# Last expert of a mixture-of-experts kernel: the last up stage behind two down stages, and row statistics taken half by half

## The chip, the cores and the metric

The kernel runs on one core of a Trainium2 chip. The metric is the time of the whole program on the device in microseconds, the median of several runs. The profile shows one further execution of the same program.

## What is computed

Two transformer layers on 256 tokens of 1024 features. The first has a gated delta network and a dense feed-forward part; the second has windowed attention and a mixture of eight experts. The change lies in the mixture and in the layer norm behind it. Of the reference, what matters is:

```python
for e in range(N_EXPERTS):                      # 8 experts, EXPERT_DIM = 3584
    h = jax.nn.silu(xf @ w_gate[e]) * (xf @ w_up[e])
    out = out + gates[:, e:e + 1].astype(xf.dtype) * (h @ w_down[e])
...
x = layer_norm(ALPHA * x + f, ln_g[i, 1], ln_b[i, 1])
```

The gates of a token are nonzero for the two experts with the largest router logits.

## The kernel before

All matmuls of the experts work on weights in fp32, each of which is split on the core into a rounded part `hi` and a remainder `lo`. The function `unit` does this for one piece of 1 MB: a transfer from the SyncE queue into a `raw` buffer (line 145), a cast to `hi` on ScalarE (line 154), and the subtraction `lo = raw - hi` on VectorE (line 155). `raw` buffers come from a ring, of which eight are in use in the last expert; `hi` and `lo` have four buffers each.

Up to 128 tokens are gathered for each expert. Its 3584 inner features are worked on in seven blocks of 512, numbered 0 to 6 (`NB` is 7). A block has a gate stage, an up stage and a down stage, and each of these stages needs two units of weights. The blocks go in pairs, (0,1), (2,3), (4,5), and the last alone. The list `stages` holds the order: gate and up of a pair, then the down stages of the pair before it, then an entry "held" that does the work which needs the finished gate and up sums. So the last expert ends with

```python
gate 6, up 6, down 4, down 5, held 6, down 6      # and then finish(7)
```

`work` is the same list without the "held" entries. Each stage first calls `loads` for the next stage of `work`, so weights are asked for one stage ahead. In the up stage the gate sum goes through Silu on ScalarE into `msg` (line 1363). Where an expert has at most 64 tokens, which is the branch that these runs take from the second expert on (`light` in `arms`), the `hi` and `lo` parts of the tokens lie side by side (`xp`, `hp`), the matmul of line 1205 does both, and the two halves of a sum are added by a copy `low` (line 1199) and a matmul with `fold` (line 1195). `multiply` forms `msg * up` on VectorE (line 1329); `turned` transposes the product on TensorE (line 1253), casts it to `hT` on ScalarE (1256), subtracts on VectorE (1257) and packs both into `hp` on ScalarE (1118, 1119), which the down stage reads. `turn_one` does this for one block of the list `held`.

The results of the other experts are gathered into `yt` (line 1292, POOL queue) and added to `y` on VectorE (line 1294) by `collect`; its second half is called with `issue_after(subs[-1].ins)`, which puts it behind the last subtraction written so far on VectorE. `finish` adds the last expert to `y` without that detour: casts `yh`, subtractions `yl`, matmuls with `PT` (1285, 1286), and four updates of `y` (1288), one for each block of 128 tokens and each half of the features. Then a branch follows (`tc.If(cv > P)`, line 1404), for experts with more than 128 tokens, which these runs don't enter. Behind it come the row statistics of `y` (`bn_stats` 1470, `bn_aggr` 1471), the reciprocal root, and the scaled output in four pieces.

The order of instructions on each engine is set when the program is built: by the order in which they are written, by the buffers that are free, and by a planner's own costs.

Of the kernel before, what the change touches and what calls it, by code (L numbers as in the profile page):

```python
# [23 lines left out]
F32 = mybir.dt.float32  # L24
# [6 lines left out]
P = 128  # L31
# [8 lines left out]
NE = 8  # L40
# [42 lines left out]
def kernel(ctx: ExitStack, tc: tile.TileContext, A, out):  # L83
    nc = tc.nc
    V, S, G, PE = nc.vector, nc.scalar, nc.gpsimd, nc.tensor
# [999 lines left out]
    def at(j, tb):  # L1085
        return bass.IndirectOffsetOnAxis(ap=keyi[:, j, tb:tb + 1], axis=0)

    with ExitStack() as mctx:
        ylng = [raw_in(per, t) for t in ("Bh", "lngb")]
        turns = more_ring(mctx, "ring_m", 2, [raw_in(per, t) for t in ("Al", "Bl", "Ah")] + ylng)  # L1090
# [139 lines left out]
        def down(e, b, hT, us, then=lambda: None):  # L1230
            if b == 0:
                acc[e] = [accb() for _ in range(2)]

            def heavy():
                for u, (wh, wl) in enumerate(us):
                    for h in range(2):
                        mm3(acc[e][h], lambda k: hT[0][:, 0, (2 * u + k) * P:(2 * u + k + 1) * P],
                            lambda k: hT[0][:, 1, (2 * u + k) * P:(2 * u + k + 1) * P],
                            [(wh[:, k, h * 512:(h + 1) * 512], wl[:, k, h * 512:(h + 1) * 512]) for k in range(2)],
                            b == 0 and u == 0, b == NB - 1 and u == 1)  # L1240

            def light():
                for u, ws in enumerate(us):
                    for h in range(2):
                        mm2(acc[e][h], hT[1], 2 * u, [[w[:, k, h * 512:(h + 1) * 512] for k in range(2)] for w in ws],
                            b == 0 and u == 0, b == NB - 1 and u == 1)
                then()
            arms(e, heavy, light)
# [23 lines left out]
        def finish(e):  # L1272
            PT = mp.tile([P, T], F32R, name="PT", bufs=1)
            p = trb()
            for tb in range(2):
                PE.transpose(p[:, tb * P:(tb + 1) * P], Pe[e][:, tb, :], ident)
            S.copy(PT, p[:, :T])
            for h in range(2):
                yh = mp.tile([P, 512], F32R, name="yh", tag="msg")
                yl = mp.tile([P, 512], F32R, name="yl", tag="low")  # L1280
                S.copy(yh, acc[e][h])
                V.tensor_sub(yl, acc[e][h], yh.bitcast(F32))
                for tb in range(2):
                    p = trb()
                    PE.matmul(p, PT[:, tb * P:(tb + 1) * P], yh, start=True, stop=False)
                    PE.matmul(p, PT[:, tb * P:(tb + 1) * P], yl, start=False, stop=True)
                    ys = y[tb][:, h * 512:(h + 1) * 512]
                    V.scalar_tensor_tensor(ys, p, gate[:, tb, e:e + 1], ys, op0=OP.mult, op1=OP.add)

        def collect(j, tb):  # L1290
            yt = per.tile([P, D], F32, name="yt", tag="x%d" % tb)
# [13 lines left out]
        def loads(what, e, b):  # L1305
            if what == "down":
                behind[0] = None
                v = wd_[e].rearrange("(f p) n -> p f n", p=P)
                return [unit(v[:, 4 * b + 2 * u:4 * b + 2 * u + 2, :], 2, D) for u in range(2)]
            w = (wg_ if what == "gate" else wu_)[e]  # L1310
            behind[0] = placed if (e, b) == (0, 1) or (e, b, what) == (0, 0, "up") else None
            if b == NB - 1:
                return colunits(w, 512 * b, 512)
            k0, c0 = 4 * (b % 2), 1024 * (b // 2)
            v = w.rearrange("(k p) n -> p k n", p=P)
            return [unit(v[:, k0 + 2 * u:k0 + 2 * u + 2, c0:c0 + 1024], 2, 1024) for u in range(2)]

        work = [s for s in stages if s[0] != "held"]
        nexts = iter(work[1:])
        hT, held, mine, late, kept = {}, [], [], [], None  # L1320
        ready = {work[0]: loads(*work[0])}

        def turn_one():
            e, b, s = held.pop(0)
            hT[e, b] = turned(s, e)
# [6 lines left out]

        for what, e, b in stages:
            if what != "held":
                nxt = next(nexts, None)
                quanta[0] = 1 if e or b > 1 else 4
                if nxt:
                    ready[nxt] = loads(*nxt)
                us = ready.pop((what, e, b))
            whole = b == NB - 1 or b % 2  # L1340
            if what == "gate":
                if b % 2 == 0:
                    pgs = [mm() for _ in range(1 if whole else 2)]
                gateup(e, b, us, pgs)
                if b % 2 == 0 and b < NB - 1:
                    multiply()
                elif held:
                    turn_one()
                if whole:
                    lgs_ = [low(p) if e else None for p in pgs]  # L1350
                if kept is not None and (e, b) == (kept[0] + 1, 2):
                    next(kept[1], None)
                    kept = None
            elif what == "up":
                if b % 2 == 0:
                    pus = [up() for _ in range(1 if whole else 2)]
                gateup(e, b, us, pus, lambda: [addlow(p, l) for p, l in zip(pgs, lgs_)] if whole else None)
                if held:
                    turn_one()
                if whole:  # L1360
                    for n, (pg, pu) in enumerate(zip(pgs, pus)):
                        s_ = mp.tile([P, 512], F32, name="msg", tag="msg")
                        S.activation(s_, pg, AF.Silu)
                        mine.append((b - len(pgs) + 1 + n, pu, low(pu) if e else None, s_, e))
                if b == 1 and e + 1 < NE:
                    fetch(e + 1)
                if b == 5 - 2 * (e > 0) and e + 1 < NE:
                    xg[e + 1] = gather(e + 1)
            elif what == "held":
                if e:  # L1370
                    arms(e, lambda: None, lambda: [addlow(pu, lu_) for _, pu, lu_, _, _ in mine])
                if b == NB - 2 or (e, b) == (NE - 1, NB - 1):
                    multiply()
                if (e, b) == (NE - 1, NB - 1):
                    turn_one()
                if (e, b) == (NE - 2, NB - 1):
                    turns.remove(ylng[0])
                    yy = per.tile([P, 2, D], F32, name="y", tag="Bh")
                    for tb in range(2):
                        y.append(yy[:, tb])  # L1380
                        nc.gpsimd.dma_start(y[tb], x3d[tb * P:(tb + 1) * P])
                        G.tensor_scalar(y[tb], y[tb], ALPHA, None, op0=OP.mult)
                if e == NE - 1 and b > 1:
                    with tc.issue_after(subs[-1].ins):
                        for c in late:
                            next(c, None)
                    late = [collect(b // 2 - 1, tb) for tb in range(2)] if b < NB - 1 else []
                    for c in late:
                        next(c)
                if (e, b) == (NE - 1, 1):  # L1390
                    turns.remove(ylng[1])
                    lnp = ln_params(3, nc.gpsimd)
                if (e, b) == (NE - 1, 5):
                    onehot(e, True)
            else:
                down(e, b, hT.pop((e, b)), us)
                if b == NB - 1 and e < NE - 1:
                    kept = (e, keep(e))
                    next(kept[1])
        finish(NE - 1)  # L1400


    cv = nc.values_load(cnti[0:1, 0:1], min_val=0, max_val=T)
    with tc.If(cv > P):
        with tc.For_i(0, E, 1) as ei, ExitStack() as octx:
# [51 lines left out]
            for h in range(2):  # L1457
                S.copy(y2[:, h * 512:(h + 1) * 512], ya[h])
                for tb in range(2):
                    p = trb()  # L1460
                    PE.matmul(p, PT2[:, tb * P:(tb + 1) * P], y2[:, h * 512:(h + 1) * 512], start=True, stop=True)
                    ys = y[tb][:, h * 512:(h + 1) * 512]
                    V.scalar_tensor_tensor(ys, p, pse[:, 2, tb:tb + 1], ys, op0=OP.mult, op1=OP.add)

    g, b = lnp
    mv = small.tile([P, 2, 2], F32, name="fin_mv")
    for tb in range(2):
        st = small.tile([P, 2, 6], F32, name="ln_st")
        for h in range(2):
            V.bn_stats(st[:, h, :], y[tb][:, h * 512:(h + 1) * 512])  # L1470
        V.bn_aggr(mv[:, tb, :], st)  # L1471
    ve, rs = (small.tile([P, 2], F32, name="fin_" + n) for n in ("ve", "rs"))
    V.tensor_scalar(ve, mv[:, :, 1], LN_EPS, None, op0=OP.add)  # L1473
    rsqrt(rs, ve, [P, 2])
# [29 lines left out]
```

## Time and profile before

| | |
|---|---|
| time, median of 3 runs | 1416.77 us (1416.58 to 1417.6) |
| profiled execution, its own time | 1412.96 us |
| its span | 1411.3 us |
| mean granted TensorE clock | 0.988 of full speed |
| busy share PE, PEld, DVE, ACT, POOL | 93%, 74%, 83%, 72%, 5% |

The span is what the profile covers; the profiled execution's own time also has what lies around it. PE is TensorE's matmuls, PEld its weight loads, DVE VectorE, ACT ScalarE, POOL GpSimd, SP SyncE; a "q" behind the name is the engine's queue of transfers. Times in rows are counted from the start of the span.

### The profile page before, as it was taken

What the parts mean: (1) busy time and instruction counts of PE and PEld (TensorE: products, weight loads), DVE (VectorE), ACT (ScalarE), POOL (GpSimd) and SP (SyncE); (2) the same over time, 40 slices, a digit from 0 to 9 for tenths busy, and PEclk for the clock granted to TensorE, in tenths of its full rate; (3) what the DMA queues carried; (4) which work ended last, traced back from release to release, by engine and by line L of the source; (5) the groups of instructions that cost most, each with busy time, mean ns of one, the idle gap of its engine ahead of it and who ended that gap; (6) DMA issues with size and microseconds to landing.
All of it is one profiled execution on the core that took longest, in us unless ns stands there. A gap on an engine that the chain in (4) does not pass through costs nothing. (4 is left out here: it accounts for less than half of the span.)

```text
span 1411.3 us, 17398 instructions
## 1 busy us (share of the span) xinstructions
PE 1309.4 (93%) x6175; PEld 1042.5 (74%) x6175; DVE 1165.8 (83%) x1300; ACT 1013.4 (72%) x1264; POOL 67.3 (5%) x90
## 2 busy tenths in 40 slices
PE   7999999999999999988999999998989999888884
PEld 5889788888777888766677777776667776666662
DVE  4885975554877898889988888889998889999998
ACT  4763544444364577799888878789988888998983
POOL 4000000000000320000000000000000000002110
PEclk9999999999999899999999999999999999999998
DMA  8641576764643899999999999999999999999992
GB/s 272 199 151 61 180 260 220 236 209 151 203 174 117 306 421 415 362 397 404 419 410 378 353 368 359 359 372 409 405 419 416 357 375 380 395 414 418 419 416 80
DMA packets 145378, 446.76 MB, mean 317 GB/s; under 512 B 12704, under 2 KB 20032, under 8 KB 145264
## 3 DMA queue, kind: packets, MB, share of 16 engines
q1 hardware_dynamic: 137072, 420.64, 78.3%
q0 software_dynamic: 5280, 18.66, 3.5%
q10 hardware_dynamic: 2912, 5.90, 1.3%
q8 instruction: 76, 1.25, 0.3%
q14 instruction: 38, 0.31, 0.1%
HBM read 435.05 MB, written 15.36 MB: 319 GB/s over the span
## 5 line engine op out<-in xcount | busy, mean ns | idle before, releaser
L155 DVE TENSOR_TENSOR lo<-raw,hi 128x2048 fp32r<-128x2048 f32 (+1 forms) x610 | 910.2, 1534 | 115.8 <-ACT hi L154 111.8
L154 ACT CAST hi<-raw 128x2048 fp32r<-128x2048 f32 (+1 forms) x610 | 769.5, 1312 | 152.5 <-PE acc L171 59.1
L1205 PE MATMUL acc<-lo,xp 128*128 128x512 f32 x224 | 74.6, 420 | 18.7 <-DVE lo L155 16.4
L170 PE MATMUL acc<-hi,hT 128*128 128x512 f32 x224 | 88.4, 395 | 2.0 <-ACT hi L154 2.0
L170 PE MATMUL mm<-hi,xg 128*128 128x512 f32 x224 | 87.5, 392 | 0.5 <-ACT low L1199 0.5
L170 PE MATMUL acc<-hi,xg 128*128 128x512 f32 x224 | 88.0, 393 | 0.0
L171 PE MATMUL mm<-hi,xg 128*128 128x512 f32 x224 | 87.3, 390 | 0.0
L171 PE MATMUL acc<-hi,hT 128*128 128x512 f32 x224 | 87.3, 390 | 0.0
L171 PE MATMUL acc<-hi,xg 128*128 128x512 f32 x224 | 87.2, 389 | 0.0
L1205 PE MATMUL mm<-lo,xp 128*128 128x512 f32 x224 | 70.7, 403 | 10.2 <-DVE lo L155 10.1
L1205 PE MATMUL acc<-lo,hp 128*128 128x512 f32 x224 | 71.5, 400 | 4.5 <-DVE lo L155 4.4
L1205 PEld LDWEIGHTS acc<-lo,xp 128*128 128x128 f32 x224 | 38.8, 190 | 45.1 <-DVE lo L155 39.1
L1205 PE MATMUL acc<-hi,hp 128*128 128x512 f32 x224 | 70.7, 397 | 1.2 <-ACT hp L1119 1.2
L1205 PE MATMUL mm<-hi,xp 128*128 128x512 f32 x224 | 68.7, 393 | 2.2 <-ACT low L1199 1.5
L1205 PE MATMUL acc<-hi,xp 128*128 128x512 f32 x224 | 69.7, 398 | 0.0
L173 PE MATMUL acc<-lo,hT 128*128 128x512 f32 x224 | 69.0, 389 | 0.0
L173 PE MATMUL acc<-lo,xg 128*128 128x512 f32 x224 | 67.7, 389 | 0.0
L173 PE MATMUL mm<-lo,xg 128*128 128x512 f32 x224 | 67.7, 389 | 0.0
L1329 DVE TENSOR_TENSOR msg<-msg,acc 128x512 f32<-128x512 f32 x56 | 36.5, 684 | 36.0 <-PEq L1189 33.1
L1205 PEld LDWEIGHTS mm<-lo,xp 128*128 128x128 f32 x224 | 40.3, 188 | 27.3 <-DVE lo L155 19.9
L1118 ACT CAST hp<-tr 128x256 fp32r<-128x256 f32 x49 | 19.0, 387 | 55.0 <-DVE hT L1257 54.9
L1253 PE MATMUL tr<-ident,msg 128*128 128x128 f32 x224 | 34.9, 284 | 22.6 <-DVE msg L1329 22.6
(410 smaller groups left out, 2325.6 us busy)
## 6 DMA issues: line engine op xcount, KB each, us to landing
raw<-in_moe_w_gate_dram SPq DMA_DIRECT2D x112, 1024.0 KB, 7.8
raw<-in_moe_w_up_dram SPq DMA_DIRECT2D x112, 1024.0 KB, 7.5
raw<-in_moe_w_down_dram SPq DMA_DIRECT2D x112, 1024.0 KB, 8.0
raw<-in_a_w_in_dram SPq DMA_DIRECT2D x12, 1024.0 KB, 5.6
raw<-in_ffn_w_gate_dram SPq DMA_DIRECT2D x11, 1024.0 KB, 5.0
raw<-in_ffn_w_up_dram SPq DMA_DIRECT2D x11, 1024.0 KB, 5.1
raw<-in_ffn_w_down_dram SPq DMA_DIRECT2D x11, 1024.0 KB, 4.9
raw<-in_b_w_in_dram SPq DMA_DIRECT2D x5, 1024.0 KB, 5.1
```

The lines of the kernel that those rows point to most:

```text
L154: S.copy(hi[:, c], raw[:, c])
L155: subs.append(V.tensor_sub(lo[:, c], raw[:, c], hi[:, c].bitcast(F32)))
L170: PE.matmul(ps, xh(k), wh, start=first and k == 0, stop=False)
L171: PE.matmul(ps, xl(k), wh, start=False, stop=False)
L173: turn[0] = PE.matmul(ps, xh(k), wl, start=False, stop=last and k == n - 1)
L1118: S.copy(v[:, :, 0], p)
L1205: PE.matmul(ps, x[:, (k0 + i % n) * P:(k0 + i % n + 1) * P], w, start=first and i == 0, stop=last and i == 2 * n - 1)
L1253: PE.transpose(p[:, f * P:(f + 1) * P], s[:, f * P:(f + 1) * P], ident)
L1329: V.tensor_mul(s_, s_, pu)
```

## The change

In the last expert the up stage of block 6 is taken out of its place and put behind the down stages of blocks 4 and 5: gate 6, down 4, down 5, up 6, held 6, down 6. The order in which weights are asked for is changed as well: gate 6, down 4, down 6, down 5, up 6, so the two units of down 6 are split ahead of those of down 5, and up 6's come last of all. Since `work` no longer has the order of `stages`, the loop asks for weights until those of the stage at hand are there. Both blocks 4 and 5 are turned in the gate stage, and the second pair of `y` additions from `collect` is written behind the down stage of block 5. The `bn_stats` of `y` are written directly behind each update of `y`, in `finish` and in the branch that isn't entered, and `bn_aggr` stands ahead of the branch (and at its end). A tile `st` and a small unused tile join the pool `rt`.

```diff
+    mv = small.tile([P, 2, 2], F32, name="fin_mv")
+    st = rt.tile([P, 2, 2, 6], F32, name="fin_st")
+    rt.tile([P, 8], F32, name="pad")
...
                     V.scalar_tensor_tensor(ys, p, gate[:, tb, e:e + 1], ys, op0=OP.mult, op1=OP.add)
+                    V.bn_stats(st[:, tb, h, :], ys)
...
+        end = NE - 1, NB - 1
+        at_up = stages.index(("up",) + end)
+        stages.insert(at_up + 2, stages.pop(at_up))
         work = [s for s in stages if s[0] != "held"]
+        work.insert(-2, work.pop())
...
             if what != "held":
-                nxt = next(nexts, None)
                 quanta[0] = 1 if e or b > 1 else 4
-                if nxt:
-                    ready[nxt] = loads(*nxt)
+                while True:
+                    nxt = next(nexts, None)
+                    if nxt:
+                        ready[nxt] = loads(*nxt)
+                    if (what, e, b) in ready:
+                        break
                 us = ready.pop((what, e, b))
...
                 elif held:
+                    turn_one()
+                if (e, b) == end:
                     turn_one()
...
                 down(e, b, hT.pop((e, b)), us)
+                if (e, b) == (NE - 1, NB - 2):
+                    with tc.issue_after(subs[-1].ins):
+                        for c in late:
+                            next(c, None)
+                    late = []
...
         finish(NE - 1)
+
+    def means():
+        for tb in range(2):
+            V.bn_aggr(mv[:, tb, :], st[:, tb])
+
+    means()
...
                     V.scalar_tensor_tensor(ys, p, pse[:, 2, tb:tb + 1], ys, op0=OP.mult, op1=OP.add)
+                    V.bn_stats(st[:, tb, h, :], ys)
+        means()
...
-    mv = small.tile([P, 2, 2], F32, name="fin_mv")
-    for tb in range(2):
-        st = small.tile([P, 2, 6], F32, name="ln_st")
-        for h in range(2):
-            V.bn_stats(st[:, h, :], y[tb][:, h * 512:(h + 1) * 512])
-        V.bn_aggr(mv[:, tb, :], st)
```

## Rows read from the trace of the kernel before

In rows of instructions the columns are: start, length in us from the first start to the last end, engine, line, operation, output and inputs, and in brackets the engine's idle time before it and what ended it.

**Rows 1.** The page, busy time of each engine over the span with its share and its number of instructions.

```profile
PE 1309.4 (93%) x6175; PEld 1042.5 (74%) x6175; DVE 1165.8 (83%) x1300; ACT 1013.4 (72%) x1264; POOL 67.3 (5%) x90
```

**Rows 2.** Busy time by stretch, near the end: stretch, its length, busy us of PE, PEld, DVE, ACT, POOL with numbers of instructions, granted clock, share of the transfer engines, GB/s.

```profile
1360.00:1380.00 20.00, 14.96 (x63) 10.78 (x61) 20.00 (x19) 13.83 (x14) 4.22 (x2) 1.00 1.01 411
1380.00:1400.00 20.00, 12.86 (x53) 8.96 (x53) 18.71 (x21) 9.14 (x12) 0.00 (x0) 0.95 0.03 11
```

**Rows 3.** The last run of weight transfers that the SyncE queue issues, in order of time, and a shorter stretch of the table by stretch.

```profile
1354.07 13.17 SPq L145 DMA_DIRECT2D raw<-in_moe_w_down_dram  x6
...
1380.00:1384.00 4.00, 2.76 (x14) 2.11 (x15) 4.00 (x5) 4.00 (x5) 0.00 (x0) 1.00 0.12 47
```

**Rows 4.** VectorE in order of time, 1366 to 1393.

```profile
1366.76 2.48 DVE L1294 SCALAR_TENSOR_TENSOR y<-yt,gat,y 128x1024 f32<-128x1024 f32 x2
...
1372.06 2.29 DVE L155 TENSOR_TENSOR lo<-raw,hi 128x2048 fp32r<-128x2048 f32 x1
...
1382.38 0.69 DVE L1329 TENSOR_TENSOR msg<-msg,acc 128x512 f32<-128x512 f32 x1
...
1387.38 0.70 DVE L1257 TENSOR_TENSOR hT<-tr,hT 128x512 fp32r<-128x512 f32 x1
1387.98 2.29 DVE L155 TENSOR_TENSOR lo<-raw,hi 128x2048 fp32r<-128x2048 f32 x1
1390.18 2.49 DVE L1294 SCALAR_TENSOR_TENSOR y<-yt,gat,y 128x1024 f32<-128x1024 f32 x2
```

**Rows 5.** TensorE's matmuls in order of time: the last up stage (1372 to 1376) and the last down stage (1388 to 1393).

```profile
1372.07 1.19 PE L1205 MATMUL acc<-lo,xp 128*128 128x512 f32 x4 [3.06 <-DVE lo L155]
...
1374.40 1.19 PE L1205 MATMUL acc<-lo,xp 128*128 128x512 f32 x4 [0.22 <-DVE lo L155]
1375.44 0.40 PE L1195 MATMUL mm<-low,fold 128*128 128x512 f32 x1
...
1388.84 0.73 PE L1205 MATMUL acc<-hi,hp 128*128 128x512 f32 x2 [1.20 <-ACT hp L1119]
1389.41 0.63 PE L1205 MATMUL acc<-lo,hp 128*128 128x512 f32 x2
...
1392.15 0.62 PE L1205 MATMUL acc<-lo,hp 128*128 128x512 f32 x2
```

**Rows 6.** ScalarE in order of time: an `hT` cast of an earlier block, a weight cast, and the way of the last up stage.

```profile
1304.12 0.59 ACT L1256 CAST hT<-tr 128x512 fp32r<-128x512 f32 x1 [0.93 <-PE tr L1253]
...
1371.63 1.94 ACT L154 CAST hi<-raw 128x2048 fp32r<-128x2048 f32 x1
...
1380.03 0.60 ACT L1363 ACTIVATE msg<-mm 128x512 f32<-128x512 f32 x1
1380.51 0.59 ACT L1199 CAST low<-acc 128x512 fp32r<-128x512 f32 x1
...
1388.11 0.37 ACT L1118 CAST hp<-tr 128x256 fp32r<-128x256 f32 x1 [0.82 <-DVE hT L1257]
1388.38 0.41 ACT L1119 CAST hp<-hT 128x256 fp32r<-128x256 f32 x1
```

**Rows 7.** TensorE and VectorE in order of time: an addition of `low` that had to wait for it, the step from two additions over two multiplies to transposes, and the last transposes of a product.

```profile
1305.25 0.50 PE L1195 MATMUL acc<-low,fold 128*128 128x512 f32 x1 [0.34 <-ACT low L1199]
...
1357.80 0.61 PE L1195 MATMUL acc<-low,fold 128*128 128x512 f32 x2
...
1358.36 1.28 DVE L1329 TENSOR_TENSOR msg<-msg,acc 128x512 f32<-128x512 f32 x2
...
1359.10 1.25 PE L1253 MATMUL tr<-ident,msg 128*128 128x128 f32 x8 [0.69 <-DVE msg L1329]
...
1383.12 0.66 PE L1253 MATMUL tr<-ident,msg 128*128 128x128 f32 x4 [1.12 <-DVE msg L1329]
```

**Rows 8.** The tile `yt` from 1290 on: the gathers on POOL (their length as minimum, median and maximum in ns, first and last start) and the time from an issue of this tile's transfers to landing.

```profile
L1292 POOL DMA_INDIRECT yt<-ys,keyi x4: 1751/1922/2470, 1316.6 to 1370.4; - x4
...
DMA to landing us min/median/max: 7.5/8.9/9.9
```

**Rows 9.** VectorE in order of time, from the updates of `y` in `finish` to the last scale.

```profile
1394.03 1.40 DVE L1288 SCALAR_TENSOR_TENSOR y<-tr,gate,y 128x512 f32<-128x512 f32 x2
1395.66 1.41 DVE L1288 SCALAR_TENSOR_TENSOR y<-tr,gate,y 128x512 f32<-128x512 f32 x2 [0.23 <-PE tr L1286]
1397.97 1.88 DVE L1470 BATCH_NORM_STATS2 ln_st<-y 128x6 f32<-128x512 f32 x3 [0.90 <-DVEq L1404]
1399.77 0.19 DVE L1471 BATCH_NORM_AGGREGATE fin_mv<-ln_st 128x2 f32<-128x12 f32 x1
...
1400.44 0.73 DVE L1478 SCALAR_TENSOR_TENSOR y<-y,fin_mv,lngb 128x512 f32<-128x512 f32 x1
...
1405.31 2.74 DVE L1479 SCALAR_TENSOR_TENSOR y<-y,fin_rs,lngb 128x512 f32<-128x512 f32 x4
```

**Rows 10.** Busy time by stretch where the granted clock (the third column from the right) fell: columns as in Rows 2.

```profile
28.00:30.00 2.00, 0.00 (x0) 0.00 (x0) 0.00 (x0) 0.00 (x0) 1.49 (x7) 0.81 0.10 36
...
462.00:464.00 2.00, 1.08 (x5) 1.11 (x6) 1.95 (x6) 0.00 (x0) 0.27 (x1) 0.69 1.03 406
```

**Rows 11.** TensorE in order of time: the first matmuls behind these two gaps.

```profile
30.14 1.02 PE L429 MATMUL acc<-g__261,cst 128*128 128x8 f32 x4 [3.44 <-POOL g__261 L425]
...
462.92 1.94 PE L1003 MATMUL tr<-ident,x 128*128 128x128 f32 x8 [2.46 <-DVE x L312]
```

## The prediction

> **What bounds the kernel now.** I read the page first: over the whole span TensorE (PE) has the largest busy share, 93% [rows 1], which alone would suggest counting matmuls. But the change touches only the last expert, so I went to the busy time by stretch of the last 70 us [rows 2]. There the picture turns over: from 1360 on VectorE (DVE) is busy 20.00 of 20 us and then 18.71 of 20, while PE falls to 14.96 and 12.86. The transfers are nearly as full as DVE up to 1380 and then stop: the share is 1.01, then 0.03. So the next question was when the last weights arrive. The SyncE queue issues its last run of weights in a stretch that ends at 1367.24, and the DMA share has fallen to 0.12 over 1380 to 1384 [rows 3]: the last weights are there at about 1381. The last `lo` subtraction (line 155), however, runs at 1387.98 and ends at 1390.27 [rows 4]. DVE is some nine microseconds behind the memory. In the end stretch the stream of `lo` subtractions on DVE, one of about 2.2 us for each unit of weights (start to start; 2.29 us each), sets the pace, and PE waits for them (3.06 us before the last up stage) [rows 5].
>
> What follows the last subtraction is short. The last down stage is 16 matmuls from 1388.84 to 1392.77 [rows 5]; they were released by the casts of `hp` at 1388.79 [rows 6], and the last `lo` is needed only near their end. So from the end of the last subtraction to the end of the last down matmul pass only 1392.77 - 1390.27 = 2.50 us. Two down stages' worth of subtractions hide the long way from the last up stage to `hp`: on DVE the multiply `msg` (line 1329) stands at 1382.38 and the `hT` subtraction at 1387.38, among the weights [rows 4].
>
> **Part 1, the order of stages and weights.** Number of matmuls, casts, subtractions and weight transfers is unchanged, and the transfers' 1 MB units are equal, so the SyncE queue does the same waits at the same slots and the last landing stays at about 1381. What changes is what is last: now the two units of the last up stage. After their last subtraction nothing may start until this chain is through, and no weights are left to hide it. Each link from its own row:
>
> 1. Four `lo` matmuls and the addition of the gate's `low`. Today the subtraction at 1372.06 ends at 1374.35 [rows 4] and the addition (line 1195) ends at 1375.84 [rows 5]: 1.49 us.
> 2. Silu and the cast of `low` on ScalarE, one behind the other: 1380.03 to 1381.10, 1.07 us [rows 6]; with a release of about 0.08 us, 1.15.
> 3. Addition of the up `low`: 0.05 us of release and 0.50 [rows 7]: 0.55.
> 4. Multiply: 0.69 us [rows 4]. The pair of multiplies at 1358.36 starts 0.17 us after the first of its two additions must have ended (1357.80 + 0.39) [rows 7], so 0.87 with that release.
> 5. Four transposes: from the multiply's end at 1383.07 to 1383.12 + 0.66: 0.71 [rows 4, 7].
> 6. `hT` cast 0.59 us with 0.03 of release [rows 6]: 0.62; `hT` subtraction 0.70 [rows 4] with 0.04: 0.74.
> 7. `hp`, two casts, 1388.08 to 1388.79 [rows 4, 6]: 0.71.
> 8. The 16 down matmuls, 1388.79 to 1392.77 [rows 5, 6]: 3.98.
>
> Sum: 10.82 us, against 2.50 today: **+8.32**. The cover of links 2 to 7 was DVE's and ScalarE's work on down weights; with it gone they cost their full length.
>
> The subtraction stream itself also moves. On DVE, which takes its instructions in order, the multiply (0.60 from start to start) and the `hT` subtraction (0.60) leave the stream for the chain behind it; the second pair of `y` accumulations (line 1294, 1390.18 to 1392.57, 2.39) [rows 4] is put behind the subtractions of the second down stage, and so ahead of the last up stage's two, which queue behind it. Their gather is issued at 1370.4 on POOL and done issuing at about 1372.8, and that isn't moved; with up to 9.9 us to land [rows 8] it is ready at about 1382.7, ahead of its new place at about 1384.6. Net **+1.19**. From below: if the accumulations fall into the chain's idle time after all, the stream gains 1.20 instead, but then a slot wait appears (next paragraph), and the net is about 0. I take +1.19, since the first pair, too, stands today where it is written, at 1366.76 and ahead of the up stage's subtractions [rows 4].
>
> Slots: `hi` and `lo` have four buffers each, and the weights of the last down stage now hold two until the end. The last up's units must wait until the second down stage has read its own. After the first of that stage's subtractions, six matmuls of 0.23 us [rows 5] and a cast of 1.94 us [rows 6] make 3.4 us before the first up subtraction can begin. Behind it on DVE stand one subtraction (2.2) and the accumulations (2.39), 4.6 us together: covered. Without the accumulations it would be a wait of 1.2 us. Two `hT` instead of one are turned in the gate stage; their work is the same and its place is not on the last path. I take 0.
>
> **Part 2, row statistics.** The four `bn_stats` after the branch (three take 1.88 us from 1397.97) [rows 9] move behind each `y` update in `finish`. They were and are on DVE, on the path. Before: first update at 1394.03 to start of the scale by `rs` at 1405.31, 11.28 us [rows 9], of which 0.23 is a wait for PE and 0.90 the branch. After: four updates of 0.66 and four statistics of 0.605 start to start, 5.06; two aggregates 0.30; the branch 0.90; the rest of the chain 4.87 (1400.44 to 1405.31) less one aggregate, 4.76. Sum 11.02: **-0.26**. The branch cannot be hidden by it. Bounds: 0 if the branch takes longer, -1.5 if the statistics fit into waits.
>
> **Sum.** 8.32 + 1.19 - 0.26 = +9.25. The profiled execution took 1412.96 us (span 1411.3), so 1422.2; its time stands 3.8 us under the median of the runs, 1416.77, which gives **1426.0**.
>
> **Rivals.**
>
> *A. The clock falls in the new gap (slower still).* Between the last up matmuls and the down matmuls PE now has about 1.2 us of work in 5.3. The granted clock fell from full speed, 2.4 GHz, towards 1.2 GHz (a mean of 0.81 over 28 to 30) after PE had been idle for 3.44 us up to 30.14, and it fell between 462 and 464, after small matmuls and 2.46 us of idleness [rows 10, 11]. Against it: it stayed at 1.00 through the idle 3.06 us before the last up stage (no stretch from 1360 to 1380 is lower) and through 1380 to 1384 with 2.76 of 4 us busy [rows 2, 3, 5]. If it falls, the 16 matmuls at 0.228 from start to start (twelve in 2.74 us) [rows 5] take twice that, +3.65, and the last few of `finish` some 0.35: 1430.0. The Trainium skill ("TensorE: Matmul & The Clock Gate", "HAM oscillation") says that a matmul burst after an idle wait starts at the low clock and that each such burst pays; by that rule the sum would be this rival's 1430.0 and not 1426.0. The rows above show both outcomes after gaps of this size.
>
> *B. Slots run short.* If ScalarE's queue delays the casts of the last units (it already waits for DVE's `hT` subtractions ahead of `hp`) [rows 6], the waits bounded at 1.2 us above come on top, at most twice that with the accumulations: 1427.2 to 1428.4.
>
> *C. Not slower: PE's waits were the loss.* From 1368 on PE stands idle for 3.06 us before the up stage and for 1.20 us before the last down stage [rows 5]. If both go because down matmuls fill them, and the end is PE's, the time is 1416.8 - 4.3 - 0.3 = 1412.2. That needs the last subtraction to end some 13.5 us earlier than I have it (9.25 + 4.3), at about 1378, before the last weights have landed (1381). Even if DVE followed the memory at once, landing at 1381, a cast, a subtraction and 10.82 us of chain end at 1396, still 3.3 us behind today's 1392.77. What would save it is that the chain is shorter than its links, below 7.5 us, as well as DVE free.
>
> *D. The order isn't followed.* The order on each engine is set when the kernel is built, and not as written throughout: the eight transposes of two blocks run in one piece at 1359.10 [rows 7], where the code asks for one block in the gate stage and for the other in the up stage. If the up weights are still split ahead of the down weights, the time stays at about 1416.5. Against it: there are only four buffers and the down weights ask first.
>
> **Chances and range.** My sum 0.55; A 0.22; B 0.09; C 0.06; D 0.08. That gives faster 0.06, same (within 0.2%, 2.8 us, about what measurement can tell from no change) 0.08, slower 0.86. My sum's own uncertainty is -2.5 (statistics in waits, accumulations in the gap) to +1.5. The range reaches over A: 1420.0 to 1431.5, and on the low side some way towards D.
>
> **What would show it.** In the profile after: the last line-155 subtraction belongs to an up stage and ends at about 1391.5; DVE is then idle for more than 2 us before a lone multiply; the last 16 down matmuls begin about 6.8 us later and end near 1402; the clock there is 1.00 (sum) or 0.50 (A); no `bn_stats` stands behind the branch. The prediction is wrong if the subtraction stream ends before 1385, if the chain's links overlap with weight work, or if DVE waits ahead of the last two units (B).

## The result

The changed kernel takes 1435.93 us (median; 1435.25 to 1436.71) against 1416.67 of the kernel before in the same comparison: 1.0146 times the time, with a 95% interval of 1.0123 to 1.0169. That is 19.3 us slower, where 9.25 were forecast, and 4.4 us above the range. The two profiled executions stand further apart than the medians, 1411.3 and 1434.9 us of span, since that of the kernel before lay 3.7 us under its median and that of the changed kernel 0.8 over its own; so positions are compared within the profiles below, and prices by medians.

The page of the changed kernel, span and busy times; [rows 1] is the second line's counterpart:

```profile
span 1434.9 us, 17394 instructions
...
PE 1331.2 (93%) x6175; PEld 1049.9 (73%) x6175; DVE 1166.3 (81%) x1300; ACT 1012.0 (71%) x1264; POOL 64.8 (5%) x90
```

The number of instructions on TensorE and VectorE is the same to the piece. VectorE's busy time is the same to half a microsecond. TensorE's has grown by 21.8 us with the same 6175 matmuls: they last longer. The next views say which.

**First place: long before the edited stages.** VectorE in order of time, four multiplies `msg` in the middle of the program, first in the kernel before:

```profile
690.82 0.68 DVE L1329 TENSOR_TENSOR msg<-msg,acc 128x512 f32<-128x512 f32 x1
...
936.17 0.69 DVE L1329 TENSOR_TENSOR msg<-msg,acc 128x512 f32<-128x512 f32 x1 [2.88 <-PEq L1189]
...
1044.48 0.68 DVE L1329 TENSOR_TENSOR msg<-msg,acc 128x512 f32<-128x512 f32 x1
...
1273.78 0.68 DVE L1329 TENSOR_TENSOR msg<-msg,acc 128x512 f32<-128x512 f32 x1
```

and the same four multiplies in the changed kernel:

```profile
694.36 0.68 DVE L1338 TENSOR_TENSOR msg<-msg,acc 128x512 f32<-128x512 f32 x1
...
945.15 0.69 DVE L1338 TENSOR_TENSOR msg<-msg,acc 128x512 f32<-128x512 f32 x1 [3.41 <-PEq L1192]
...
1053.57 0.68 DVE L1338 TENSOR_TENSOR msg<-msg,acc 128x512 f32<-128x512 f32 x1
...
1285.62 0.68 DVE L1338 TENSOR_TENSOR msg<-msg,acc 128x512 f32<-128x512 f32 x1
```

The changed kernel is late by 3.54, 8.98, 9.09 and 11.84 us. On every engine the instructions stand in the same order in both kernels up to the last expert, so nothing was moved there. Most of the lag grows in some experts only: the trace has matmuls with `xg` and `hT`, the branch for more than 64 tokens, in experts 0, 2, 3 and 5, and there it grows, by 10.7 us in all; with `xp` and `hp`, in experts 4, 6 and 7, it stays to within 0.2. (Ahead of the prediction it is said that these runs take the short branch from the second expert on. That was wrong: four of the eight take the long one.)

In expert 1, a short one, the lag grows by 1.67 us too, and that has nothing to do with the change. It is TensorE's clock, first in the kernel before, then in the changed one (columns as in [rows 2]):

```profile
608.00:610.00 2.00, 2.00 (x10) 1.65 (x10) 2.00 (x2) 0.17 (x1) 0.00 (x0) 1.00 1.04 420
```

```profile
608.00:610.00 2.00, 2.00 (x6) 1.52 (x6) 2.00 (x2) 1.06 (x1) 0.00 (x0) 0.52 0.95 332
```

Of all the traces of this case only that of the kernel before has full speed there; the others, also those in which nothing is displaced, lose 1.5 to 1.7 us at this place. Ahead of the first expert the changed kernel is 0.8 us early. So 10.7 of the 11.84 are the experts of the long branch, and the rest lies between these two executions.

TensorE's matmuls by line and operands in the stretch 820 to 920, which lies in such experts; the last figures before the idle time are busy us and mean ns. The kernel before:

```profile
L171 PE MATMUL acc<-hi,xg 128*128 128x512 f32 x48 | 18.7, 389 | 0.0
...
L171 PE MATMUL acc<-hi,hT 128*128 128x512 f32 x40 | 15.6, 390 | 0.0
```

The changed kernel:

```profile
L171 PE MATMUL acc<-hi,xg 128*128 128x512 f32 x48 | 18.9, 393 | 0.0
...
L171 PE MATMUL acc<-hi,hT 128*128 128x512 f32 x39 | 15.3, 393 | 0.0
```

The same matmul lasts a little longer. From start to start, over all neighbouring matmuls with `xg` in the trace, the median went from 227 to 232 ns (means 227.1 and 232.6), and with `hT` likewise. An expert of the long branch has 42 units with 12 matmuls each, 504 x 0.0055 = 2.8 us; the lag grows by 2.6 to 2.7 in each of the four.

**Second place: the end.** VectorE in order of time in the changed kernel, to be read against [rows 4, 9]:

```profile
1370.20 1.28 DVE L1338 TENSOR_TENSOR msg<-msg,acc 128x512 f32<-128x512 f32 x2
...
1396.42 2.47 DVE L1298 SCALAR_TENSOR_TENSOR y<-yt,gat,y 128x1024 f32<-128x1024 f32 x2
1398.82 4.70 DVE L155 TENSOR_TENSOR lo<-raw,hi 128x2048 fp32r<-128x2048 f32 x2
1406.84 0.69 DVE L1338 TENSOR_TENSOR msg<-msg,acc 128x512 f32<-128x512 f32 x1 [3.33 <-PE acc L1198]
1408.90 0.69 DVE L1260 TENSOR_TENSOR hT<-tr,hT 128x512 fp32r<-128x512 f32 x1 [1.37 <-ACT hT L1259]
...
1417.92 1.40 DVE L1291 SCALAR_TENSOR_TENSOR y<-tr,gate,y 128x512 f32<-128x512 f32 x2
...
1428.97 2.74 DVE L1500 SCALAR_TENSOR_TENSOR y<-y,fin_rs,lngb 128x512 f32<-128x512 f32 x4
```

The order is as written: the second pair of sums `y`, the two subtractions of the last up stage, then a lone multiply behind 3.33 us of idle time. The multiply of blocks 4 and 5 at 1370.20 stood at 1358.36 before [rows 7]: that is the lag of 11.84 that the kernel brings into its end. TensorE in order of time over the same stretch, against [rows 5]:

```profile
1403.57 1.21 PE L1208 MATMUL acc<-lo,xp 128*128 128x512 f32 x4 [0.29 <-DVE lo L155]
1404.61 0.40 PE L1198 MATMUL mm<-low,fold 128*128 128x512 f32 x1
1406.26 0.47 PE L1198 MATMUL acc<-low,fold 128*128 128x512 f32 x1 [1.26 <-ACT low L1202]
1407.59 0.66 PE L1256 MATMUL tr<-ident,msg 128*128 128x128 f32 x4 [0.85 <-DVE msg L1338]
...
1410.35 1.22 PE L1208 MATMUL acc<-hi,hp 128*128 128x512 f32 x2 [1.89 <-ACT hp L1122]
...
1415.57 0.62 PE L1208 MATMUL acc<-hi,hp 128*128 128x512 f32 x2
1416.03 0.63 PE L1208 MATMUL acc<-lo,hp 128*128 128x512 f32 x2
```

and busy time by stretch there, columns as in [rows 2]:

```profile
1406.00:1408.00 2.00, 0.89 (x5) 0.60 (x6) 0.69 (x1) 0.12 (x1) 0.00 (x0) 1.00 0.00 0
1408.00:1410.00 2.00, 0.46 (x5) 0.22 (x3) 0.69 (x1) 1.24 (x4) 0.00 (x0) 0.66 0.00 0
1410.00:1412.00 2.00, 1.65 (x4) 1.36 (x5) 0.00 (x0) 0.30 (x1) 0.00 (x0) 0.50 0.00 0
```

Between the last up matmuls and the down matmuls TensorE has short pieces of work with waits of 1.26, 0.85 and 1.89 us between them, and in the last of these the granted clock goes from 1.00 to 0.50, 1.2 GHz. The down matmuls begin at half speed and end at full speed: 1410.35 to 1416.66, 6.31 us, where [rows 5] show 3.93.

Measured from the multiply of blocks 4 and 5, the last subtraction ends 1.41 us later than before (1403.52 - 11.84 = 1391.68, against 1390.27). From there to the end of the last down matmul pass 13.14 us instead of 2.50, +10.64. From there to the end of the span (1434.91, and 1411.26 before) pass 18.25 instead of 18.49, -0.24. Together +11.81 for the end, and with the 11.84 that came before it 23.65, the difference of the spans.

### The profile page after: what moved, and what is told of

It is laid out like the page before. It is cut to its first block, busy times and chain, and to the rows that moved or that the text cites. A ratio compares the mean times of both kernels' runs of the same rounds, so it can differ in the third digit from the quotient of the medians.

```text
span 1434.9 us, 17394 instructions
## 1 busy us (share of the span) xinstructions
PE 1331.2 (93%) x6175; PEld 1049.9 (73%) x6175; DVE 1166.3 (81%) x1300; ACT 1012.0 (71%) x1264; POOL 64.8 (5%) x90
## 5 line engine op out<-in xcount | busy, mean ns | idle before, releaser
L1208 PE MATMUL acc<-lo,hp 128*128 128x512 f32 x224 | 75.1, 418 | 8.0 <-DVE lo L155 7.9
L1208 PE MATMUL acc<-hi,hp 128*128 128x512 f32 x224 | 75.1, 418 | 4.3 <-ACT hi L154 2.4
L1208 PEld LDWEIGHTS acc<-lo,hp 128*128 128x128 f32 x224 | 42.9, 198 | 24.7 <-DVE lo L155 15.5
```

The lines of the kernel that those rows point to most:

```text
L1208: PE.matmul(ps, x[:, (k0 + i % n) * P:(k0 + i % n + 1) * P], w, start=first and i == 0, stop=last and i == 2 * n - 1)
```

## The experiments

In the expectations S is the theory that a shift of addresses did it, D that any displacement does, M that matmuls are slowed by where their stationary operand lies, O that the new order of stages did, W that the order of weights did, A that the low clock did, and R that executions just differ. The kernel before, run beside each, took 1414.2 to 1415.1 us.

**What moves up when `st` and the unused tile join the pool `rt`.** They take 96 and 32 bytes of each partition, 128 together, and pools opened later lie above them. By the addresses given when the program is built, `xg` went from 180736 to 180864, `hT` from 201728 to 201856, `xp` and `hp` likewise, and the ring `ring_m` too; `hi`, `lo` and `raw`'s other ring stayed. Before, these were multiples of 256 bytes (and of 512), and then odd multiples of 128. So the first kernel is the one before with 128 bytes more in `rt` and nothing else:

```diff
+    rt.tile([P, 32], F32, name="pad")
     with ExitStack() as mctx:
```

> The kernel before with one unused tile of 128 bytes per partition in the pool rt, and nothing else: every tile of the pools above it (ring_m, moe) lies 128 bytes higher, as in the changed kernel, and the order of all instructions is that of before. Theory S (the shift of addresses costs the 7 to 12 us that the changed kernel has lost before the last expert's tail begins): 1424 to 1428.5 us, matmuls of the experts slower by some 2%, the last part as before. Rival O (the reordered stages cost it all, in a way that shows before them): 1416.7 us. Rival R (the executions differ among themselves, not the programs): 1416.7 us as well, with the kernel before drifting by several us.

Measured: 1424.41 us, 1.0075 [1.0049, 1.0100], +10.2. In its trace the lag grows by 10.8 us in the experts of the long branch, and stands at 10.25 at the multiply of blocks 4 and 5. An unused tile makes about half of the loss.

Next, the 128 bytes between the ring and the experts' own pool, so that only the latter moves:

```diff
     turns = more_ring(mctx, "ring_m", ...)
+    mctx.enter_context(tc.tile_pool(name="between", bufs=1)).tile([P, 32], F32, name="pad")
```

> The kernel before with 128 unused bytes between the pools ring_m and moe: only the tiles of moe (xg, hT, xp, hp, low, msg) lie 128 bytes higher, the raw buffers where they were. Theory M (the matmuls are slowed by the place of their stationary operands xg and hT): all of the loss of the run with both pools moved, some 10 us above before, 1424 us; matmuls with xg and hT again 1 to 2% longer. Rival W (the weights' way, that is transfers into and reads out of the moved raw buffers): no change from before, about 1414.3 us.

Measured: 1424.45 us, 1.0071 [1.0047, 1.0096]. The whole loss comes from the pool that holds `xg`, `xp`, `hT` and `hp`; the ring has no part in it.

The first edit with 512 and with 256 bytes instead of 128:

```diff
+    rt.tile([P, 128], F32, name="pad")     # the second kernel: [P, 64]
```

> The kernel before with 512 unused bytes in the pool rt, so ring_m and moe lie 512 bytes higher. In the kernel before, every moe tile that TensorE reads starts at a multiple of 512 bytes of its partition, in the changed kernel none does. Theory M with alignment (what counts is whether the 512 bytes that one weight load takes from a partition straddle such a boundary): as before, about 1414.3 us. Rival D (any displacement of these pools costs): some 1424 us.

> The kernel before with 256 unused bytes in the pool rt: the moe tiles lie at odd multiples of 256 bytes. If the boundary that counts is one of 512 bytes, every weight load of 512 bytes a partition straddles one again, and the loss is that of the 128-byte run, about 10 us: 1424 us. If multiples of 256 are enough, no change: 1414.5 us. If the loss grows with the part that lies beyond the boundary, more than 10 us.

Measured: 1415.15 us, 1.0009 [0.9993, 1.0025], with 512, and 1414.97, 0.9999 [0.9989, 1.0010], with 256. So it isn't displacement as such, and multiples of 256 are enough, where I had supposed 512. The group in the trace of the kernel with 256 bytes is back at the value of before:

```profile
L171 PE MATMUL acc<-hi,xg 128*128 128x512 f32 x48 | 18.7, 389 | 0.0
```

Then 128 bytes ahead of `xg` and 128 behind it, which moves `xg` to an odd multiple of 128 and all others by 256:

```diff
+        mp.tile([P, 32], F32, name="pad0", bufs=1)
         # ... xg of the first expert is made here
+        mp.tile([P, 32], F32, name="pad1", bufs=1)
```

> The kernel before with 128 unused bytes ahead of the gathered tokens xg and 128 behind them in the pool moe: xg lies at an odd multiple of 128 bytes, hT, xp and hp at multiples of 256. If a matmul is slowed by the place of its own stationary operand: in the experts with more than 64 tokens the matmuls with xg have 0.233 us from start to start and those with hT 0.228 as before; gate and up are two thirds of these experts' matmuls, so two thirds of the 10 us: 1421 us. If any displaced tile of the pool slows all matmuls: 1424.5 us. If it is hT alone: 1414.5 us.

Measured: 1421.45 us, 1.0047 [1.0030, 1.0065], +6.5. Its groups on TensorE, 820 to 920:

```profile
L171 PE MATMUL acc<-hi,xg 128*128 128x512 f32 x48 | 19.0, 395 | 0.0
...
L171 PE MATMUL acc<-hi,hT 128*128 128x512 f32 x38 | 14.8, 390 | 0.0
```

Matmuls that take their stationary 128x128 piece from the moved tile are slow, those from `hT` in the same stretch are not. Gate and up stages read `xg`, 28 of 42 units: two thirds of 10.2 would be 6.8. That settles M for `xg`. What the hardware does differently is not settled: the weight loads themselves last 188 ns in both kernels.

**The parts of the change one by one.** The changed kernel without displacement (`st` in the place of an existing tile, no unused tile):

```diff
-    st = rt.tile([P, 2, 2, 6], F32, name="fin_st")
-    rt.tile([P, 8], F32, name="pad")
+    st = rt.tile([P, 2, 2, 6], F32, name="fin_st", tag="before")
```

> The changed kernel with its tile st put into the room of a tile of the same pool that is no longer needed, and without the unused tile, so that no address of ring_m or moe moves. Theory S: the time of before plus what the tail measured, 11.8 us by the two profiles: 1427 to 1429.5 us. Rival O: 1436 us as the changed kernel. Rival R: anything between.

Measured: 1427.65 us, 1.0090 [1.0065, 1.0116], +13.4.

The order of stages and weights alone, with the statistics as before:

```diff
...
+        stages.insert(at_up + 2, stages.pop(at_up))
...
+        work.insert(-2, work.pop())
...
+                if (e, b) == end:
+                    turn_one()
...
+                if (e, b) == (NE - 1, NB - 2):
+                    with tc.issue_after(subs[-1].ins):
+                        ...
```

> The order of stages and weights of the changed kernel, the row statistics as before, no address moved. Theory S with the terms of the prediction: 0.3 us above the run without the shift, 1427 to 1430 us. Rival O: 1436 us. If the statistics half by half cost rather than gain, this one is below the run with both.

Measured: 1425.02 us, 1.0067 [1.0044, 1.0089], +10.8, under the 1427 to 1430 expected; a second time, further down, the same kernel took 1426.88. From the end of its last subtraction to that of its last down matmul pass 13.37 us (13.14 in the changed kernel).

The statistics alone, `st` in the place of an existing tile again:

```diff
+    st = rt.tile([P, 2, 2, 6], F32, name="fin_st", tag="before")
...
+                    V.bn_stats(st[:, tb, h, :], ys)
...
+    means()
```

> The row statistics half by half alone, order of stages as before, no address moved. By the prediction's term 0.26 us below before: 1416.4 us, which is less than can be told from no change. A rival that the statistics lengthen the end (their instructions stand between the updates for which TensorE waits): 1417 to 1418.5 us.

Measured: 1415.14 us, 1.0005 [0.9991, 1.0018]; a gain of 0.26 us can't be told from none in this. In its trace the stretch behind the last down matmul takes 18.26 us, nearly the 18.25 of the changed kernel, against 18.49 before. So order and displacement are the two causes, and their prices by medians, 10.8 and 10.2, make 21.0, near the 19.3 measured for both.

The changed kernel with one number altered, the unused tile at 416 bytes, so that with `st` it makes 512:

```diff
-    rt.tile([P, 8], F32, name="pad")
+    rt.tile([P, 104], F32, name="pad")
```

> The changed kernel with one number altered: the unused tile of rt has 416 bytes instead of 32, so that st and it make 512 and the moe tiles begin at multiples of 512 bytes again. If the place of the moe tiles is what the changed kernel lost besides its tail: 8 to 12 us below the changed kernel, 1425 to 1428 us. If st itself or the statistics cost it: 1436 us.

Measured: 1427.09 us, 1.0079 [1.0060, 1.0098]. 8.8 us of the loss are back.

**The end.** These kernels are that of the order alone with one further edit. First, the weights of the two last down stages in the order of their blocks:

```diff
-        work.insert(-2, work.pop())
```

> The run with the order of stages alone, but with the weights asked for in the order of the stages (gate 6, down 4, down 5, up 6, down 6), so that the last two subtractions are down weights again. By the terms of the prediction the chain behind the last up weights then starts 4.4 us earlier on VectorE and is covered up to the multiply: the end comes 3.2 us sooner than with the order of stages alone, 1421 to 1422.5 us, and the clock may not fall. Rival: the chain from the up weights is what costs, and not what follows in the stream, so no change, 1425 us.

Measured: 1422.1 us (1420.11 to 1424.95), 1.0057 [1.0038, 1.0077], 2.9 under the order alone. In the traces the way from the multiply of blocks 4 and 5 to the end of the last down matmul is 43.37 us, against 47.13 in the order alone. VectorE in order of time:

```profile
1387.28 4.48 DVE L155 TENSOR_TENSOR lo<-raw,hi 128x2048 fp32r<-128x2048 f32 x2
1391.69 0.68 DVE L1333 TENSOR_TENSOR msg<-msg,acc 128x512 f32<-128x512 f32 x1
```

The last down stage's subtractions are again last and cover the way to the multiply. The clock falls all the same (0.67 over 1390 to 1392, then 0.50), and the 16 matmuls take 6.4 us.

Next, the second pair of sums `y` in its old place, behind the last subtraction:

```diff
-                if (e, b) == (NE - 1, NB - 2):
-                    with tc.issue_after(subs[-1].ins):
-                        ...
-                    late = []
```

> The run with the order of stages alone, but the second pair of accumulations of y stays where the kernel before has it, behind the last subtraction, so in the idle time of VectorE in the new chain. By the prediction's terms the subtractions end 2.39 us earlier less a wait of 1.2 us for buffers: 1.2 us below the order alone, about 1423.8 us, with VectorE idle for about 1.2 us ahead of the last two subtractions. If the buffers are not short: 2.4 us below. If the accumulations are late and hold up the multiply: above 1425 us.

Measured: 1426.99 us, 1.0080 [1.0062, 1.0098]: no gain. The time is that of the third forecast, but the accumulations hold up nothing: the multiply waits for TensorE. VectorE in order of time:

```profile
1385.19 4.49 DVE L155 TENSOR_TENSOR lo<-raw,hi 128x2048 fp32r<-128x2048 f32 x2
1391.58 2.29 DVE L155 TENSOR_TENSOR lo<-raw,hi 128x2048 fp32r<-128x2048 f32 x1 [1.90 <-ACT hi L154]
1394.61 2.29 DVE L155 TENSOR_TENSOR lo<-raw,hi 128x2048 fp32r<-128x2048 f32 x1 [0.74 <-ACT hi L154]
1396.82 2.48 DVE L1294 SCALAR_TENSOR_TENSOR y<-yt,gat,y 128x1024 f32<-128x1024 f32 x2
1400.22 0.69 DVE L1334 TENSOR_TENSOR msg<-msg,acc 128x512 f32<-128x512 f32 x1 [0.93 <-PE acc L1195]
```

The last two subtractions now wait 1.90 and 0.74 us for their casts, which wait for buffers that TensorE still reads. Busy time by stretch in the same kernel, columns as in [rows 2], tells part of why they are read so late:

```profile
1386.00:1388.00 2.00, 0.47 (x1) 0.47 (x2) 2.00 (x2) 0.32 (x1) 0.00 (x0) 0.50 0.12 45
1388.00:1390.00 2.00, 2.00 (x6) 1.52 (x6) 1.68 (x1) 0.35 (x1) 0.00 (x0) 0.50 0.00 0
```

TensorE is at half speed there, too: ahead of the first of the two casts, which starts at 1389.64, five down matmuls take 2.11 us from 1387.53 on, where at 0.23 each they would take some 1.15 (an estimate). That is the wait for slots which the prediction put at 1.2 us for this case; it is 2.64, and it takes back the 2.39 of the sums.

Next, filler matmuls to keep TensorE busy in the gap, on operands that are at hand: four behind each of the two additions of `low`, seven ahead of the last down stage. Their result is never used.

```diff
+        def idle(n):
+            for _ in range(n):
+                PE.matmul(spare[0], fold, xg[NE - 1].rearrange("p l k c -> p (l k c)")[:, :512], start=True, stop=True)
```

> The run with the order of stages alone, with 15 matmuls of 512 columns put into the gaps of TensorE between the last up matmuls and the last down matmuls; their results are not used. Theory A (the low clock that the profiles show in the last down matmuls comes from these gaps, and costs the chain 2.3 us): granted clock 1.00 there, the 16 down matmuls in 3.9 us rather than 6.2, and 2 to 2.5 us less than with the order alone: 1422 to 1423.5 us. Rival: the clock falls anyway, or the fillers delay the chain by what they save: 1425 us or more.

Measured: 1425.33 us (1424.57 to 1428.11), 1.0085 [1.0058, 1.0112], beside 1425.02 for the order alone, not told apart. In the trace the clock stays at 1.00, though, and the way from the last subtraction to the last down matmul is 11.17 us. Both kernels were therefore timed again, beside each other and with more executions:

> The order of stages alone, a second time, beside the run with fillers: 1425 to 1427 us.

> The order of stages with the 15 filler matmuls, a second time, in the same call. If the low clock costs time: 2 to 2.5 us below the run without fillers. If not: the same.

Measured: 1426.88 us (1425.92 to 1429.26), 1.0090 [1.0074, 1.0105], for the order alone, and 1423.70 (1423.15 to 1425.38), 1.0063 [1.0049, 1.0076], with the fillers: 3.2 us less for fifteen matmuls of useless work. TensorE's last down stage, first without fillers:

```profile
1400.12 1.22 PE L1205 MATMUL acc<-hi,hp 128*128 128x512 f32 x2 [1.89 <-ACT hp L1119]
...
1406.06 0.63 PE L1205 MATMUL acc<-lo,hp 128*128 128x512 f32 x2
```

then with them:

```profile
1401.23 0.74 PE L1205 MATMUL acc<-hi,hp 128*128 128x512 f32 x2 [0.29 <-ACT hp L1119]
...
1404.58 0.61 PE L1205 MATMUL acc<-lo,hp 128*128 128x512 f32 x2
```

6.57 us without, 3.96 with. The way from the last subtraction to the last down matmul is 13.39 us without and 11.18 with: the fillers delay the start of the down matmuls by 0.4 and save 2.6 behind it. So the low clock comes from the gap, and by the traces it costs 2.2 us net of the fillers' own delay. The end explains no more than that of the 3.2; the first pair, timed in two different sets of executions, showed no gain.

Last, a test of whether VectorE's stream sets the end at all: the kernel before with the sums `y` on GpSimd.

```diff
-            V.scalar_tensor_tensor(y[tb], yt, gat2[:, j, tb:tb + 1], y[tb], op0=OP.mult, op1=OP.add)
+            G.tensor_scalar(yt, yt, gat2[:, j, tb:tb + 1], None, op0=OP.mult)
+            G.tensor_tensor(y[tb], y[tb], yt, op=OP.add)
...
-                    with tc.issue_after(subs[-1].ins):
-                        ...
                     for c in late:
                         next(c)
+                    for c in late:
+                        next(c, None)
```

> The kernel before with the accumulations of gathered rows into y done on GpSimd (a scale and an addition for each), so that VectorE loses the 2.39 us of the first pair out of its stream ahead of the last up weights, and the second pair behind it. If VectorE's stream of subtractions sets the end of the kernel, as the prediction read it, the last subtraction ends 2.4 us sooner and the time falls by some 2.4 us: 1411.8 us. If TensorE or the transfers set it, no change: 1414.2 us. If GpSimd's work slows VectorE's while both run, up to 2 us above before.

Measured: 1421.07 us, 1.0040 [1.0026, 1.0055], 6 us slower, three times the most that was expected. VectorE while GpSimd works:

```profile
1345.73 25.43 DVE L155 TENSOR_TENSOR lo<-raw,hi 128x2048 fp32r<-128x2048 f32 x8
```

and GpSimd in the same trace:

```profile
1350.50 6.16 POOL L1294 TENSOR_SCALAR yt<-yt,gat 128x1024 f32<-128x1024 f32 x1
1356.75 2.60 POOL L1295 TENSOR_TENSOR y<-y,yt 128x1024 f32<-128x1024 f32 x1
1359.32 7.00 POOL L1294 TENSOR_SCALAR yt<-yt,gat 128x1024 f32<-128x1024 f32 x1
```

Eight subtractions take 3.2 us each in the mean, where they take 2.2 [rows 4]; singly, three of them still last 2.28 and the longest 4.50. VectorE got rid of 4.8 us of sums and lost some 8 in this one run of subtractions. The Trainium skill ("GPSIMD Engine Reference", "Specifications") says that GpSimd shares its SBUF interfaces with VectorE and gets in the way of instructions there that have two inputs in SBUF; the trace agrees, with 2.2 us turned into 3.2 in the mean. The end moves with VectorE's stream, as [rows 2, 4] were read: the stream's loss before the multiply of blocks 4 and 5 comes out at the end, less 2.07 us behind it, where the first pair of sums [rows 4] is gone.

None of these kernels beats the one before.

## Why the prediction was wrong

- **The step that failed** is the sentence that isn't there: the prediction lists what the change removes, adds and moves, and leaves out what the tile `st` and the unused tile beside it displace. It priced two tiles at nothing without saying so. They cost 10.2 us by themselves (1424.41 against 1414.26), through matmuls of experts that the diff doesn't touch. The diff showed both tiles; the question of what lies above them in the same memory was not asked. [Rows 5] could not show it: they hold durations at one placement only.
- **Links 1 to 7 of the chain** hold. Last subtraction to first down matmul: 6.83 us, forecast 10.82 - 3.98 = 6.84. Each link alone is within 0.1 us: 1.49 (1.49), Silu to the addition's end 1.72 (1.70), multiply 0.80 (0.87), transposes 0.72 (0.71), `hT` 1.34 (1.36), `hp` 0.76 (0.71).
- **Link 8** is mis-sized: 6.31 us and not 3.98. This is rival A, which had 0.22: the clock fell in the gap. Its mechanism was right and its price of 3.65 too high, since the clock is back for the last four matmuls and nothing in `finish` is slower: 2.33. What I held against it was one execution: in its trace the clock stayed up behind the 3.06 us of waiting before the last up stage [rows 2, 5]. In all six other traces of kernels with that order of stages, the statistics alone and the five with shifted addresses, it falls behind that same wait. In the kernel with 512 bytes more:

```profile
1380.00:1382.00 2.00, 2.00 (x6) 1.52 (x6) 2.00 (x2) 0.00 (x0) 0.00 (x0) 0.50 1.02 412
```

It costs nothing there, since VectorE sets the pace: the last subtraction ends 31.9 us after the multiply of blocks 4 and 5 in all seven traces. So the low chance of A rested in part on a row that does not repeat. The Trainium skill ("TensorE: Matmul & The Clock Gate", "HAM oscillation") was the better guide: it tells of matmuls that start at the low clock behind each wait, for waits on transfers that are longer than the three here. The traces agree: the last down matmuls start at half speed in the changed kernel, in the order alone and with the weights in order of blocks.
- **The subtraction stream**: +1.41, forecast 1.19. The missing 0.2 are slots, taken at 0: the last two subtractions take 4.70 us as a pair, where other pairs take 4.49. In the two traces of the order alone the stream ends 1.85 and 1.89 later, and the last subtraction waits for its cast there (0.57 in the first). That the sums cover the wait was right, and with the sums moved away the bound of 1.2 for it was too low (2.64). The bound was reckoned with matmuls at 0.23 us, and TensorE ran part of that stretch at the low clock.
- **Statistics**: -0.24, forecast -0.26.
- **The other rivals** did not happen. B is the 0.2 above. C: VectorE's stream sets the end, not TensorE's waits. D: the order on VectorE and TensorE is the one written.

So the sum for the end, 9.25, with what rival A and the slots cost here, gives 11.8, and the changed kernel without displacement measured +13.4, its order alone +10.8 and +11.9. That would have lain in the range. The rest of the 19.3 is the displacement.

## What to carry over

A tile added to a kernel is never free until it is known what lies above it: look at which operands move, and keep stationary operands of matmuls at multiples of 256 bytes in a partition; padding of a few hundred bytes gave back 8.8 us here. Put last the stage with the shortest way to the end, even if all engines do the same amount of work either way, and count the clock when a chain of short steps between engines leaves TensorE little to do. When the loss is larger than the forecast, first find where along the program it grows, before the edited place is explained.

## What was not expected of the hardware

- 512-column fp32 matmuls follow each other at 0.227 us with the stationary operand at a multiple of 256 bytes and at 0.232, 2.4% slower by the means, at an odd multiple of 128. Only shifts by 128, 256 and 512 bytes were tried; smaller offsets stay open, and so does the mechanism.
- Fifteen filler matmuls, about 4 us of TensorE's time in the gap, made the program 3.2 us shorter where both kernels ran beside each other, of which the traces show 2.2 at the end.
- The same instructions behind the same wait of 3.06 us ran at full speed in one execution and at half speed in six others: one trace doesn't tell whether the clock falls in a gap.
- A per-partition scaling of 128x1024 in fp32 takes 4.9 to 7.0 us on GpSimd while VectorE works beside it, and VectorE's subtraction of 128x2048 goes from 2.2 to 3.2 us in the mean meanwhile.
